# Layer 0's LayerNorm statistics: from 32-column fp32 sums that are spread afterwards to full fp32r products of split sums

## The chip, the core and the metric

The kernel runs on one core of a Trainium2 chip. The metric is device time in microseconds (us) of one launch, as the median of several runs. The core has five engines that work at the same time, each through its own instruction queue in order: TensorE (PE, matmuls, with weight loads beside them), VectorE (DVE), ScalarE (ACT), GpSimd (POOL) and SyncE (SP, which issues the transfers).

## The reference

The program is one inference step of a decoder with two layers, over 256 prompt tokens and 8 sample tokens, 264 in all, with 1024 features. Layer 0 is a gated short convolution, layer 1 block-sparse attention. Each layer has a wide input projection, a mixer, an output projection, and then a LayerNorm over the features of `alpha * x + mixer(x)`:

```python
def _layernorm(x, g, b):
    xf = x.astype(jnp.float32)
    mu = xf.mean(-1, keepdims=True)
    var = jnp.square(xf - mu).mean(-1, keepdims=True)
    return ((xf - mu) * lax.rsqrt(var + LN_EPS) * g + b).astype(x.dtype)

for i in range(DEPTH):            # DEPTH = 2
    ...                           # yp, ys: the mixer's output, after the output projection
    xp = _layernorm(DN_ALPHA * xp + yp, ln_g[i], ln_b[i])
    xs = _layernorm(DN_ALPHA * xs + ys, ln_g[i], ln_b[i])
```

The change is in the LayerNorm between layer 0 and layer 1.

## The kernel before

**Layout.** Activations lie with features on the 128 partitions and tokens along the row: `xf[:, m]` holds features 128m to 128m+127 of all 264 tokens, for m = 0 to 7. So a mean over features is a sum over 8 blocks and then over partitions, and the second part needs a matmul with a constant matrix.

**Slabs.** The weights come as slabs numbered 4 to 79, each 128 output columns by 1024 inputs. A slab is loaded (`load`, line 112, on SP), and split into a high part in the fp32r format (`hi`, line 124, on ACT) and the remainder (`lo`, line 129, on DVE). Activations are split in the same way into a pair of tiles, `pair[0]` or `pair[1]` (m0h, m0l, m1h, m1l in the profile). The product of a slab is 8 blocks of three matmuls (lines 136 to 138: high x high, high x low, low x high), accumulated in one of three PSUM tiles `acc`. Slabs 32 to 39 are layer 0's output projection; slabs 40 to 71 are layer 1's input projection, 40 to 47 of it q.

**Order.** PE's order is the program's order. The work of the other engines is hung into slots by hand: `at(n, phase, f)` adds `f` to slot n, and `begin(n)`, called ahead of slab n's matmuls, issues the slot's work in the order "dma", "pe", "s0", "hi", "lo", "s1a", "s1b", "s1", "s1c"; `split_late(n)` then issues the phases "hi3" and "lo3". Two tables, `hi_slot` and `lo_slot`, say in which slot a slab is split. Slabs 45 to 49 are split in the late phases. With each `lo` goes the `load` of the slab four places later in the list of slabs, since it takes the raw tile that `lo` frees. So for slab 45 `lo` carries `load(49)`, for slab 46 `load(50)`, for slab 47 `load(51)`.

**The norm of layer 0** (class `Norm`, object `ln`). As the output slabs come in, DVE adds them to `xf` (`evac`, line 280; a shift by block 0's mean is added too), ACT squares each block (`square`, line 301), ACT and DVE form the split pair of `gamma * x` (`cg_h`, line 501; `cg_l`, line 504), and POOL adds blocks 0 to 6 and their squares up in `sr` and `q` (`sums`, lines 308 and 309). `stats_mm` (line 317) then multiplies `sr`, `q`, block 7 and its square by an fp32 constant of 32 columns, in four quarters of 66 tokens, so that each quarter of the tokens has its mean and mean square on 32 partitions. `stats` makes `var`, the square root (line 330, ACT) and the reciprocal (line 331, DVE), all on 66 columns. `bcast_mm` (line 340) spreads them over all partitions by matmuls with a selection matrix, and `bcast` (lines 346 and 349) copies them out as two tiles of 264 columns: `ln.nd` (minus the mean) and `ln.rs` (one over the deviation).

**What uses the norm.** Layer 1 does not wait for it: for slabs 40 to 46 the matmuls run on the pair of `gamma * x`, with two extra columns for gamma and beta, and the norm is put on the result (`u_evac`, lines 574 to 577, on DVE; `u_fin` on ACT), which also frees the PSUM tile `acc`. From slab 47 on the matmuls take the normalised `x1`, in `pair[1]`, which DVE and ACT form block by block in slots 40 to 46 (`x1_norm`, lines 810 and 811; `x1_affine`; `x1_low`, line 819). Slots 40 and 41 are written out by hand. In slot 46 DVE rotates the sample tokens' q and copies it into `zq` (line 707); in slot 47, after half of its matmuls, PE multiplies the first cached keys by `zq` (`qk`, line 716: scores into `sd`).

Of the kernel before, what the change touches and what calls it, by code (L numbers as in the profile page):

```python
# [10 lines left out]
F32 = mybir.dt.float32  # L11
# [10 lines left out]
N = T + B  # L22
# [27 lines left out]
def build(tc, a):  # L50
# [3 lines left out]
    with ExitStack() as top:  # L54
# [91 lines left out]
        def run(n, phase):  # L146
            for f in hooks.pop((n, phase), []):
# [3 lines left out]
                   43: 36, 44: 37, 45: 40, 46: 40, 47: 43, 48: 45, 49: 46, 50: 47, 51: 48, 52: 48, 53: 49,  # L151
                   54: 49, 78: 74}
        lo_slot = {4: 3, 5: 3, 6: 3, 7: 4, 8: 5, 9: 5, 45: 40, 46: 41, 47: 44, 51: 49, 52: 49,
# [82 lines left out]
        onem = cp.tile([128, 2, 32], F32, name="onem")  # L236
        pool.memset(onem[:, 0], -1.0 / 1024)
        pool.memset(onem[:, 1], 1.0 / 1024)
        sel = cp.tile([128, 4, 128], F32, name="sel")[:, 0]
        pool.memset(sel, 0.0)  # L240
        for j in range(4):
            pool.memset(sel[32 * j:32 * j + 1], 1.0)
# [25 lines left out]

        G = N // 4

        class Norm:
# [38 lines left out]

            def stats_mm(self):
                self.mean = att_tile("ln0")
                self.e2 = att_tile("ln1")

                def acc(p, w, src, first, last):
                    for j in range(4):
                        pe.matmul(p[32 * j:32 * j + 32, 0:G], w, src[:, G * j:G * j + G],
                                  start=first, stop=last)
                acc(self.mean, onem[:, 0], self.sr, True, False)
                acc(self.e2, onem[:, 1], self.q, True, False)  # L320
                acc(self.mean, onem[:, 0], xf[:, 7], False, True)
                acc(self.e2, onem[:, 1], self.last_sq, False, True)

            def stats(self):
                self.st = self.t("st", 2 * G)
                var = self.t("var", G)
                act.copy(self.st[:, 0:G], self.mean[:, 0:G])
                act.activation(var, self.mean[:, 0:G], AF.Square)
                dve.tensor_sub(var, self.e2[:, 0:G], var)
                act.activation(var, var, AF.Sqrt, bias=epst)  # L330
                dve.reciprocal(self.st[:, G:2 * G], var)

            def bcast_mm(self):

                two = big_tile("lnb")
                ps = [two[:, 0:2 * G], two[:, 512:512 + 2 * G]] + \
                     [att_tile(f"lnb{i}")[:, 0:2 * G] for i in range(2)]
                for j in range(4):
                    q = np.s_[32 * j:32 * j + 32]
                    pe.matmul(ps[j], sel[q], self.st[q], start=True, stop=True)  # L340
                return two, ps

            def bcast(self, nm, src, c):
                two, ps = src
                t = self.t(nm)
                act.copy(t[:, 0:2 * G].rearrange("p (j r) -> p j r", j=2),
                         two.rearrange("p (j r) -> p j r", j=2)[:, :, G * c:G * c + G])
                for j in (2, 3):
                    act.copy(t[:, G * j:G * j + G], ps[j][:, G * c:G * c + G])
                return t  # L350
# [171 lines left out]
        for m in (6, 7):  # L522
            cg_l(m)
# [4 lines left out]
        with tc.tile_pool(name="l1", bufs=1) as p1, ExitStack() as late_pool:  # L528
# [448 lines left out]
            mm(ac2[0], 40, pair[0], range(0, 4), last=False)  # L977
            ln.stats_mm()
            ln.stats()
            split_late(40)  # L980
            mm(ac2[0], 40, pair[0], range(4, 7), first=False, last=False)
            begin(41, False)
            mm(ac2[1], 41, pair[0], range(0, 3), last=False)
            ps = ln.bcast_mm()
# [179 lines left out]
```

## Time and profile before

| | us |
|---|---|
| median of 3 runs (lowest to highest) | 280.36 (280.11 to 280.70) |
| the profiled execution | 280.45 |
| its span, first to last instruction | 278.7 |
| PE busy | 272.7 (98% of the span) |
| DVE busy | 195.6 (70%) |
| ACT busy | 155.3 (56%) |
| POOL busy | 59.8 (21%) |

The profile is of one execution. Lines of the trace in order of time give the start in us, the duration in us, the engine, the line of the kernel, the operation, output <- inputs, shapes and how often it came in a row; in brackets stands how long the engine had been idle before and what ended that. Lines of a group give the count, then the busy time in us, the mean of one in ns, and idle time before. Lines of a stretch give from:to, its length, and the busy time of the engine asked for. PEld is PE's weight load. Matmul durations overlap each other; the distance of two starts is what a matmul costs.

### The profile page before, as it was taken

How to read it: one execution, taken by the hardware profiler on the slowest of the kernel's cores; microseconds unless marked ns; L12 is line 12 of the kernel's file. 1: busy time of each engine (PE TensorE's matmuls, PEld its weight loads, DVE VectorE, ACT ScalarE, POOL GpSimd, SP SyncE). 2: the span in 40 equal slices, each digit the busy share in tenths (PEclk: the TensorE clock that was granted, in tenths of full speed). 3: DMA queues.
4: the chain of work that ended last, by engine and by line, in shares of the span. 5: the costliest groups of instructions: out<-in, count | busy, mean ns of one | idle time of the engine just before them, and what ended most of it. 6: DMA issues, size and time to landing. Idle time of an engine off the chain costs nothing.

```text
span 278.7 us, 6245 instructions
## 1 busy us (share of the span) xinstructions
PE 272.7 (98%) x2330; PEld 255.6 (92%) x2330; DVE 195.6 (70%) x377; ACT 155.3 (56%) x294; POOL 59.8 (21%) x130
## 2 busy tenths in 40 slices
PE   8999999999999999999999999999999999999992
PEld 5999999999999999999998997999959987988891
DVE  3868976655766768969999498498626384993745
ACT  4876564444655538557776495567746752571101
POOL 2110532020101102850311158411100030000212
PEclk9999999999999999999999999999999999999998
DMA  7985989999666876134025999999864995781012
GB/s 230 410 266 189 310 274 331 385 373 356 230 211 224 295 238 221 43 119 152 2 75 194 387 399 348 359 335 304 277 223 149 311 379 173 236 290 61 0 78 85
DMA packets 24495, 66.34 MB, mean 238 GB/s; under 512 B 3090, under 2 KB 6930, under 8 KB 24466
## 3 DMA queue, kind: packets, MB, share of 16 engines
q1 hardware_dynamic: 24178, 65.63, 67.4%
q8 instruction: 18, 0.29, 0.4%
q10 hardware_dynamic: 288, 0.33, 0.4%
q14 instruction: 11, 0.09, 0.1%
HBM read 61.55 MB, written 3.35 MB: 233 GB/s over the span
## 4 chain that ended last, share of the span: by engine, by line
PE 98%; DVE 1%; issue 0%
PE acc L136 24%; PE acc L138 24%; PE acc L137 24%; PE c L961 4%; PE sd L716 3%; PE dps L768 3%; PE acc L961 2%; PE acc L465 2%; PE acc L466 2%; PE acc L469 1%; PE so L1062 1%; PE warmp L80 1%; PE s L649 1%; PE o L688 1%; PE c1b L961 1%; PE c1c L961 1%
## 5 line engine op out<-in xcount | busy, mean ns | idle before, releaser
L124 ACT CAST hi<-raw 128x1024 fp32r<-128x1024 f32 x76 | 79.2, 1049 | 35.2 <-DMA raw<-w 22.1
L129 DVE TENSOR_TENSOR lo<-raw,hi 128x1024 fp32r<-128x1024 f32 x76 | 92.7, 1230 | 7.6 <-ACT hi L124 7.4
L138 PE MATMUL acc<-m0h,lo 128*128 128x264 f32 (+1 forms) x280 | 79.4, 284 | 0.0
L137 PE MATMUL acc<-m0l,hi 128*128 128x264 f32 (+1 forms) x280 | 79.3, 283 | 0.0
L136 PE MATMUL acc<-m0h,hi 128*128 128x264 f32 (+1 forms) x280 | 79.3, 283 | 0.0
L136 PE MATMUL acc<-m1h,hi 128*128 128x264 f32 x264 | 76.6, 290 | 0.0
L138 PE MATMUL acc<-m1h,lo 128*128 128x264 f32 x264 | 74.8, 283 | 0.0
L137 PE MATMUL acc<-m1l,hi 128*128 128x264 f32 x264 | 74.7, 283 | 0.0
L136 PEld LDWEIGHTS acc<-m0h,hi 128*128 128x128 f32 x280 | 52.7, 188 | 0.2
L138 PEld LDWEIGHTS acc<-m0h,lo 128*128 128x128 f32 x280 | 52.8, 189 | 0.0
L137 PEld LDWEIGHTS acc<-m0l,hi 128*128 128x128 f32 x280 | 52.7, 188 | 0.0
L136 PEld LDWEIGHTS acc<-m1h,hi 128*128 128x128 f32 x264 | 49.7, 188 | 1.7 <-issue 1.7
L137 PEld LDWEIGHTS acc<-m1l,hi 128*128 128x128 f32 x264 | 49.7, 188 | 0.1
L138 PEld LDWEIGHTS acc<-m1h,lo 128*128 128x128 f32 x264 | 49.7, 188 | 0.0
L421 POOL COPY uo<-up 128x10 f32<-128x10 f32 x8 | 8.0, 1002 | 66.8 <-DVE up L420 58.9
L657 DVE TENSOR_TENSOR s<-s,cst 128x256 f32<-128x256 f32 x8 | 3.4, 430 | 14.7 <-PE s L649 14.7
L799 DVE TENSOR_TENSOR gt<-z,q 128x256 f32<-128x256 f32 x8 | 3.4, 423 | 9.4 <-ACT z L796 9.4
L932 ACT ACTIVATE row<-row,epst 128x1 f32<-128x1 f32 x2 | 0.6, 295 | 16.6 <-DVE row L931 16.6
L666 ACT ACTIVATE P<-s,mx 128x128 f32<-128x128 f32 (+1 forms) x16 | 6.6, 416 | 5.6 <-DVE mx L660 5.6
L796 ACT ACTIVATE z<-acc 128x264 f32<-128x264 f32 x8 | 3.1, 391 | 11.4 <-PE acc L138 11.4
L628 POOL COPY vs<-vh 128x8 f32<-128x8 f32 x8 | 1.6, 204 | 34.9 <-ACT vh L627 34.9
L466 PE MATMUL acc<-m0l,hi 128*128 128x264 f32 x32 | 8.9, 306 | 0.0
(215 smaller groups left out, 415.4 us busy)
## 6 DMA issues: line engine op xcount, KB each, us to landing
raw<-w SPq DMA_DIRECT2D x76, 512.0 KB, 4.7
kv<-kc SPq DMA_DIRECT2D x32, 256.0 KB, 5.7
kv<-vc SPq DMA_DIRECT2D x16, 512.0 KB, 6.6
first<-first SPq DMA_DIRECT2D x6, 388.0 KB, 6.9
k_o<-kall SPq DMA_DIRECT2D x8, 132.0 KB, 5.1
v_o<-vh SPq DMA_DIRECT2D x8, 132.0 KB, 5.2
xf<-kall SPq DMA_DIRECT2D x16, 64.0 KB, 3.1
kall<-gb SPq DMA_DIRECT2D x2, 512.0 KB, 5.0
```

The source lines that it names most:

```text
L124: act.copy(his[n][sl], raws[n][sl])
L129: dve.tensor_sub(los[n][sl], raws[n][sl], his[n].bitcast(F32)[sl])
L136: pe.matmul(acc, wh, mh[:, k, 0:w], start=first and k == ks[0], stop=False)
L137: pe.matmul(acc, wh, ml[:, k, 0:w], start=False, stop=False)
L138: pe.matmul(acc, wl, mh[:, k, 0:w], start=False, stop=last and k == ks[-1])
L421: pool.tensor_copy(uo[:, f], up[:, T:N + 2])
L465: pe.matmul(accs[s], wh, mh, start=k == 0, stop=False)
L466: pe.matmul(accs[s], wh, ml, start=False, stop=False)
L666: act.activation(P[sl], s_ps[h][sl], AF.Exp, bias=mx[:, 2 + i:3 + i], scale=SCALE, accum_out=mx[:, 4 + i:5 + i])
L716: pe.matmul(s[32 * j:32 * j + 16, 0:256], zq[:, o:o + 16], kt, start=step == 0 and i == 0, stop=step == 3 and i == 3)
L768: pe.matmul(dps[0][32 * j:32 * j + 32, 512 * c:512 * c + 512], pm[b2][pg][:, j, :], kv_tiles[step, j][:, 512 * c:512 * c + 512], start=ste ...
L961: pe.matmul(acc, g[m][:, k, t], wide(d, k)[:, c0:c1], start=k == 0 and i == 0, stop=k == 7 and i == 2)
```

## The change

The statistics are formed on all 128 partitions at once, for all 264 tokens.

- POOL also adds block 7 and its square (`sums(7)`), and the two sums are split into fp32r high and low parts (`parts`: two copies on ACT, two subtractions on DVE), ahead of `cg_l(7)`.
- `stats_mm` is four matmuls of 264 columns with the constant `ones2` (-1/128 everywhere, there already): high and low part of the sum, then of the squares. They stand on PE after 7 blocks of slab 40 and 2 of slab 41 (27 matmuls); before, the sums stood after 4 blocks of slab 40 (12 matmuls), and the spreading matmuls 18 matmuls after them.
- `stats` works on 264 columns: a square, a fused multiply and subtract, the square root, a copy and the reciprocal. `bcast_mm`, `bcast` and the constants `onem` and `sel` go.
- `hi(45)` moves from slot 40 to 38 and `lo(45)` from 40 to 39; `hi(46)` moves from slot 40 to 41 and `lo(46)` from 41 to 43.

```diff
@@ -148,9 +148,9 @@
                 f()
 
         hi_slot = {4: 3, 5: 3, 6: 3, 7: 4, 8: 4, 9: 5, 10: 5, 11: 6, 38: 33, 39: 34, 40: 22, 41: 24, 42: 26,
-                   43: 36, 44: 37, 45: 40, 46: 40, 47: 43, 48: 45, 49: 46, 50: 47, 51: 48, 52: 48, 53: 49,
+                   43: 36, 44: 37, 45: 38, 46: 41, 47: 43, 48: 45, 49: 46, 50: 47, 51: 48, 52: 48, 53: 49,
                    54: 49, 78: 74}
-        lo_slot = {4: 3, 5: 3, 6: 3, 7: 4, 8: 5, 9: 5, 45: 40, 46: 41, 47: 44, 51: 49, 52: 49,
+        lo_slot = {4: 3, 5: 3, 6: 3, 7: 4, 8: 5, 9: 5, 45: 39, 46: 43, 47: 44, 51: 49, 52: 49,
                    53: 50, 54: 50, 39: 34}
 
         order = []
@@ -233,13 +233,6 @@
         pool.memset(onesf, 1.0)
         ones2 = cp.tile([128, 128], F32R, name="ones2")
         pool.tensor_scalar(ones2, onesf, -1.0 / 128, None, ALU.mult)
-        onem = cp.tile([128, 2, 32], F32, name="onem")
-        pool.memset(onem[:, 0], -1.0 / 1024)
-        pool.memset(onem[:, 1], 1.0 / 1024)
-        sel = cp.tile([128, 4, 128], F32, name="sel")[:, 0]
-        pool.memset(sel, 0.0)
-        for j in range(4):
-            pool.memset(sel[32 * j:32 * j + 1], 1.0)
 
         kv_tiles = {}
         KV = [("k", hh, b2) for hh in range(2) for b2 in range(2)] + \
@@ -266,8 +259,6 @@
                 sp.dma_start(t, a["vc"][page(2 * j + b2, c)].rearrange("o p e -> (o p) e"))
 
 
-        G = N // 4
-
         class Norm:
             def __init__(self, gi):
                 self.gi = gi
@@ -308,46 +299,35 @@
                     pool.tensor_tensor(self.sr, self.sr, xf[:, m], ALU.add)
                 pool.tensor_tensor(self.q, self.q, self.last_sq, ALU.add)
 
+            def parts(self):
+                self.part = [[lnp.tile([128, N], F32R, name=f"{c}{d}") for d in "hl"] for c in "sq"]
+
+                def high(i):
+                    act.copy(self.part[i][0], (self.sr, self.q)[i])
+
+                def low(i):
+                    dve.tensor_sub(self.part[i][1], (self.sr, self.q)[i], self.part[i][0].bitcast(F32))
+                self.sums(7)
+                high(0)
+                high(1)
+                low(0)
+                low(1)
+
             def stats_mm(self):
-                self.mean = att_tile("ln0")
-                self.e2 = att_tile("ln1")
-
-                def acc(p, w, src, first, last):
-                    for j in range(4):
-                        pe.matmul(p[32 * j:32 * j + 32, 0:G], w, src[:, G * j:G * j + G],
-                                  start=first, stop=last)
-                acc(self.mean, onem[:, 0], self.sr, True, False)
-                acc(self.e2, onem[:, 1], self.q, True, False)
-                acc(self.mean, onem[:, 0], xf[:, 7], False, True)
-                acc(self.e2, onem[:, 1], self.last_sq, False, True)
+                self.mean = att_tile("ln0")[:, 0:N]
+                self.e2 = att_tile("ln1")[:, 0:N]
+                for p, part in zip((self.mean, self.e2), self.part):
+                    for i, c in enumerate(part):
+                        pe.matmul(p, ones2, c, start=i == 0, stop=i == 1)
 
             def stats(self):
-                self.st = self.t("st", 2 * G)
-                var = self.t("var", G)
-                act.copy(self.st[:, 0:G], self.mean[:, 0:G])
-                act.activation(var, self.mean[:, 0:G], AF.Square)
-                dve.tensor_sub(var, self.e2[:, 0:G], var)
-                act.activation(var, var, AF.Sqrt, bias=epst)
-                dve.reciprocal(self.st[:, G:2 * G], var)
-
-            def bcast_mm(self):
-
-                two = big_tile("lnb")
-                ps = [two[:, 0:2 * G], two[:, 512:512 + 2 * G]] + \
-                     [att_tile(f"lnb{i}")[:, 0:2 * G] for i in range(2)]
-                for j in range(4):
-                    q = np.s_[32 * j:32 * j + 32]
-                    pe.matmul(ps[j], sel[q], self.st[q], start=True, stop=True)
-                return two, ps
-
-            def bcast(self, nm, src, c):
-                two, ps = src
-                t = self.t(nm)
-                act.copy(t[:, 0:2 * G].rearrange("p (j r) -> p j r", j=2),
-                         two.rearrange("p (j r) -> p j r", j=2)[:, :, G * c:G * c + G])
-                for j in (2, 3):
-                    act.copy(t[:, G * j:G * j + G], ps[j][:, G * c:G * c + G])
-                return t
+
+                self.nd, self.rs = self.t("n"), self.t("r")
+                act.activation(self.rs, self.mean, AF.Square, scale=0.125)
+                dve.scalar_tensor_tensor(self.rs, self.e2, -0.125, self.rs, ALU.mult, ALU.subtract)
+                act.activation(self.rs, self.rs, AF.Sqrt, bias=epst)
+                act.activation(self.nd, self.mean, AF.Copy, scale=0.125)
+                dve.reciprocal(self.rs, self.rs)
 
             def gcol(self, m):
                 return col(3 + 2 * self.gi, m)
@@ -519,8 +499,9 @@
 
         out_slabs(ln, 32, g, cg)
         cg_h(7)
-        for m in (6, 7):
-            cg_l(m)
+        cg_l(6)
+        ln.parts()
+        cg_l(7)
 
         l0.close()
 
@@ -974,21 +955,17 @@
 
             ac2 = [acc_tile() for _ in range(2)]
             begin(40, False)
-            mm(ac2[0], 40, pair[0], range(0, 4), last=False)
+            mm(ac2[0], 40, pair[0], range(0, 7), last=False)
+            begin(41, False)
+            mm(ac2[1], 41, pair[0], range(0, 2), last=False)
             ln.stats_mm()
             ln.stats()
             split_late(40)
-            mm(ac2[0], 40, pair[0], range(4, 7), first=False, last=False)
-            begin(41, False)
-            mm(ac2[1], 41, pair[0], range(0, 3), last=False)
-            ps = ln.bcast_mm()
-            ln.nd = ln.bcast("n", ps, 0)
-            ln.rs = ln.bcast("r", ps, 1)
             split_late(41)
             for m in (0, 1):
                 x1_norm(m)
                 x1_affine(m)
-            mm(ac2[1], 41, pair[0], range(3, 7), first=False, last=False)
+            mm(ac2[1], 41, pair[0], range(2, 7), first=False, last=False)
             for i in range(2):
                 mm(ac2[i], 40 + i, pair[0], range(7, 8), first=False)
                 at(42, "s0", u_evac, i, ac2[i])
```

## The prediction

> **What bounds the kernel now.** I read the chain of work that ended last first, then the rows of TensorE (PE), VectorE (DVE), ScalarE (ACT) and GpSimd (POOL) in order of time around layer 0's norm (118 to 146 us).
>
> ```profile
> PE 98%; DVE 1%; issue 0%
> 122.94 0.28 PE L138 MATMUL acc<-m0h,lo 128*128 128x266 f32 x1
> 123.15 0.32 PE L317 MATMUL ln<-sr,onem 128*32 128x66 f32 x8
> 123.75 0.39 PE L136 MATMUL acc<-m0h,hi 128*128 128x266 f32 x1
> 123.98 0.29 PE L137 MATMUL acc<-m0l,hi 128*128 128x266 f32 x1
> ...
> 125.97 0.28 PE L138 MATMUL acc<-m0h,lo 128*128 128x266 f32 x1
> 126.18 0.51 PE L340 MATMUL lnb<-st,sel 32*128 32x132 f32 x8
> 126.62 0.39 PE L136 MATMUL acc<-m0h,hi 128*128 128x266 f32 x1
> 126.85 0.28 PE L137 MATMUL acc<-m0l,hi 128*128 128x266 f32 x1
> ...
> 128.94 0.28 PE L136 MATMUL acc<-m0h,hi 128*128 128x266 f32 x1
> ...
> 143.68 0.28 PE L136 MATMUL acc<-m1h,hi 128*128 128x264 f32 x1
> 145.22 3.65 PE L716 MATMUL sd<-kv,zq 128*16 128x256 f32 x64
> ```
>
> PE is the chain, with hardly a gap, so whatever leaves PE in this stretch shortens the kernel unless another engine then makes PE wait. The row at 128.94 opens slab 42 and that at 143.68 slab 47: 120 matmuls in 14.74 us, 0.123 us each. The engine that could make PE wait is DVE:
>
> ```profile
> 124.79 0.57 DVE L331 RECIPROCAL st<-var 128x66 f32<-128x66 f32 x1 [0.42 <-ACT var L330]
> 125.73 2.36 DVE L129 TENSOR_TENSOR lo<-raw,hi 128x1024 fp32r<-128x1024 f32 x2 [0.37 <-ACT hi L124]
> 128.01 0.42 DVE L810 TENSOR_TENSOR xf<-xf,n 128x264 f32<-128x264 f32 x1
> 128.53 0.43 DVE L811 TENSOR_TENSOR xf<-xf,r 128x264 f32<-128x264 f32 x1
> 139.94 1.22 DVE L129 TENSOR_TENSOR lo<-raw,hi 128x1024 fp32r<-128x1024 f32 x1
> 141.07 0.15 DVE L574 COPY uv<-acc 128x2 f32<-128x2 f32 x1
> 141.26 0.49 DVE L576 SCALAR_TENSOR_TENSOR t<-n,uv,acc 128x264 f32<-128x264 f32 x1
> 143.59 0.27 DVE L707 COPY zq<-qs 128x16 f32<-128x16 f32 x2
> 128.01:143.86 15.85, 14.87 (x45) 1.00 0.31 100
> ```
>
> The last line is DVE's busy time from the first row that needs the norm's result (128.01) to the end of the copies into `zq` (143.59 + 0.27 = 143.86): 14.87 of 15.85 us. No row in it names a releaser; what is missing are steps between dependent instructions. So from 128.01 on DVE works down a queue without waiting for anybody, and PE's scores at 145.22 read `zq`, which was ready only 1.36 us earlier. That is the slack to watch.
>
> **The change, part by part.**
>
> PE, removed. The 32-column sums: 122.94 to 123.75 is 0.81 instead of 0.12, and the next step 0.23 instead of 0.12: 0.80 us. The spreading matmuls: 125.97 to 126.62 is 0.65, again followed by 0.23: 0.64 us. Together 1.44 us.
>
> PE, added. Four matmuls of 264 columns with `ones2`, of the kind that runs at 0.123 a step: 0.49 us. If nothing waits, PE gains 0.95 us. They come after 27 slab matmuls instead of 12: 121.59 (where slab 40 starts in the row below) + 27 x 0.123 = 124.91.
>
> ```profile
> 121.59 0.28 PE L136 MATMUL acc<-m0h,hi 128*128 128x266 f32 x1
> 115.09 1.49 DVE L129 TENSOR_TENSOR lo<-raw,hi 128x1024 fp32r<-128x1024 f32 x1
> 118.09 1.22 DVE L129 TENSOR_TENSOR lo<-raw,hi 128x1024 fp32r<-128x1024 f32 x1
> 119.22 0.98 DVE L504 SCALAR_TENSOR_TENSOR m0l<-xf,cst,m0h 128x264 fp32r<-128x264 f32 x1
> 120.13 0.42 DVE L280 SCALAR_TENSOR_TENSOR xf<-xf,acc 128x264 f32<-128x264 f32 x1
> 122.14 0.49 DVE L504 SCALAR_TENSOR_TENSOR m0l<-xf,cst,m0h 128x264 fp32r<-128x264 f32 x1
> 118.31 1.60 POOL L308 TENSOR_TENSOR sr<-sr,xf 128x264 f32<-128x264 f32 x1 [0.20 <-DVE xf L280]
> 119.87 0.95 POOL L309 TENSOR_TENSOR q<-q,sqm 128x264 f32<-128x264 f32 x1
> 120.78 0.75 POOL L308 TENSOR_TENSOR sr<-sr,xf 128x264 f32<-128x264 f32 x1
> 121.50 0.75 POOL L309 TENSOR_TENSOR q<-q,sqm 128x264 f32<-128x264 f32 x1
> 120.64 0.42 ACT L301 ACTIVATE sqm<-xf 128x264 f32<-128x264 f32 x1 [1.52 <-DVE xf L280]
> 124.41 0.35 ACT L330 ACTIVATE var<-var,epst 128x66 f32<-128x66 f32 x1 [0.29 <-DVE var L329]
> L124 ACT CAST hi<-raw 128x1024 fp32r<-128x1024 f32 x76 | 79.2, 1049 | 35.2 <-DMA raw<-w 22.1
> L816 ACT CAST m1h<-xf 128x264 fp32r<-128x264 f32 x8 | 3.3, 413 | 0.3
> L819 DVE TENSOR_TENSOR m1l<-xf,m1h 128x264 fp32r<-128x264 f32 x8 | 3.0, 424 | 0.0
> ```
>
> POOL and the moved `lo(45)`. A POOL sum takes 0.75 us alone (120.78), 1.60 beside a DVE `lo` (118.31); it ended 0.60 after that `lo` (118.09 + 1.22 = 119.31; 119.91). DVE's next two-input product took 0.98 instead of 0.49 and ended 0.29 after the sum (120.20), and the next sum 0.63 after that (120.83). They take turns. The Trainium skill ("SBUF — State Buffer", "SBUF: two separate sides") says that GpSimd and a VectorE instruction with two SBUF inputs hold a shared port pair in turn, for a whole instruction each; the trace agrees (1.60 against 0.75), and without turns the sum below would be that of the first rival. Before, the `sums(6)` pair at 120.78 ran at 0.75 each. Now `lo(45)` stands there, behind the evacuation at 120.13: held by the sum at 119.87 as the `lo` at 115.09 (1.49) was, it ends at 121.9. Then by turns: sum `sr` 122.5, `cg_l(6)` 122.8, sum `q` 123.4. The new `sums(7)` follow with DVE idle: 124.15 and 124.87.
>
> The splits. `high` of q: one hand-over (0.1) and a 0.41 copy (the L816 row): 125.38. `low` 0.43 (the L819 row) and 0.03: 125.84. The last stats matmul starts at 125.89 instead of 124.91 + 3 x 0.123 = 125.28: PE waits 0.61, and slab 42 opens 0.34 ahead of before.
>
> The statistics. Matmul end 126.17; DVE's fused subtract 0.42 (as L280): 126.62; the square root, 0.35 on 66 columns, about 0.54 on 264: 127.19. Then the reciprocal, 264 columns instead of 66 and still on DVE ahead of the norm:
>
> ```profile
> L671 DVE RECIPROCAL mx<-mx 128x2 f32<-128x2 f32 x8 | 1.3, 161 | 0.0
> L935 DVE RECIPROCAL row<-row 128x1 f32<-128x1 f32 x2 | 0.3, 156 | 0.0
> L329 DVE TENSOR_TENSOR var<-ln,var 128x66 f32<-128x66 f32 x1 | 0.2, 226 | 0.5 <-ACT var L328 0.5
> ```
>
> (566 - 156) / 65 = 6.3 ns a column, so 0.156 + 263 x 0.0063 = 1.81 us. Low end: 0.57 plus 198 columns at what an ordinary instruction adds, (0.424 - 0.226) / 198 = 1 ns: 0.77. High end: four times 0.566 = 2.26. I take 1.81, since the three reciprocals lie on one line. The Trainium skill ("VectorE: DVE Perf Modes", "First, the fixed hardware budget") gives the divide a repeat count of 8; at its 0.96 GHz that is an estimate of 8.3 ns a column, 2.2 us, which the slope of 6.3 ns does not bear out. So the reciprocal ends at 129.03; `x1_norm(0)` starts at 128.96 and its second product at 129.41 instead of 128.53: DVE's queue is 0.88 late.
>
> `lo(46)`. Before, both moved `lo` ran in 125.73 to 128.09, ahead of the norm. Now `lo(46)` stands in slot 43, inside the full stretch: 139.94 to 141.07, 1.13 us. At `zq` DVE is 0.88 + 1.13 = 2.01 late.
>
> The sum. `zq` is ready at 145.87, and PE's scores start at about 145.92 instead of 145.22. PE alone would be there at 144.88, so it waits 1.04, of which some 0.5 already at slab 47's start: its accumulator is the one that the L576 at 141.26 frees, now at 143.76, and PE is there at 143.34. Sum: -0.95 + 0.61 + 1.04 = **+0.70 us**. The scores themselves are 3.65 us of PE work that needs nothing more of DVE's queue, and in them the rest of its lateness is taken up.
>
> ```profile
> 126.98 1.46 SPq L112 DMA_DIRECT2D raw<-w  x2
> ```
>
> At no cost: `hi(45)` (1.05 on ACT) goes into the idle 1.52 that ACT has before 120.64; without that gap it would hold up the squares, and POOL's sums behind them, by up to 1.05. The evacuations of `n` and `r` that go, and POOL's memsets at the start, end no wait of PE. The two loads of this last row are issued by the moved `lo`: `load(49)` moves from 127 to 122, `load(50)` from 128 to 139. SP works in order, but the next in its queue, `load(51)`, waits for `lo(47)` in slot 44 anyway. Slab 50's raw tile is first read in slot 47, four microseconds later; if it landed after that, `hi(50)` would wait on ACT, and PE needs it three slabs further on.
>
> **The rivals.**
>
> 1. POOL's sums are not held up (not slower). If the `sums(6)` pair ends at 122.25 as now, `sums(7)` end at 123.85, everything up to `zq` comes 1.02 earlier, and the sum is -0.32: 280.0 us as a median. For it: the pair ran at 0.75 each. Against: `lo(45)` is queued right behind the evacuation whose result POOL waits for. It decides once q's last sum ends before 124.2 (0.70 earlier).
> 2. The reciprocal streams (0.77): `zq` late by 0.97, and PE's own 0.34 is all that is left: 280.0 us. Against: a column costs 6 ns already between 1, 2 and 66.
> 3. The reciprocal costs four times 0.566: +0.45, so +1.15: 281.5 us. For it: 8.6 ns a column at 66 columns, start-up counted in. Against: the line through 1, 2 and 66.
> 4. The whole PE gain arrives, -0.95: 279.4 us. It needs r by about 127.4, 1.6 us earlier than I have it: POOL free and a cheaper reciprocal, or room in DVE's queue that its rows do not show (its 0.98 of gaps would hold most of `lo(46)`).
>
> **How the numbers follow.** The profiled execution took 280.45 us (span 278.7 and 1.75 around it), 0.09 above the median 280.36. 280.45 + 0.70 is 281.15, as a median 281.06; I say 281.1. Under 0.2% (0.56 us) a measurement of this kernel can't tell from no change. Chances: forecast 0.45, rival 1 0.18, rival 2 0.10, rival 3 0.12, rival 4 0.15. The forecast lies just above 280.92, the bound of "slower"; I put a quarter of its chance under it. So slower is 0.34 + 0.12 = 0.46, same 0.11 + 0.28 = 0.39, faster 0.15. The range goes from rivals 1 and 2 to rival 3, 279.9 to 281.6, and leaves rival 4 out.
>
> **What would show it.** Right: POOL's `sums(6)` sum over 1.4 us beside the `lo` near 120.5; the last stats matmul half a microsecond or more behind its place; a RECIPROCAL of 128x264 at about 1.8; `x1_norm(0)` near 129; the `zq` copies ending near 145.9, the scores starting on them, and PE idle before slab 47 or the scores. Wrong: PE without a gap from slab 42 to the scores, and these ahead of 145.2. What would upset it most is an earlier r, or a DVE queue that runs faster than its rows before.

## The result, and the profile after

The changed kernel takes 281.97 us (median of 6 runs, 281.62 to 282.84); the kernel before, beside it, 280.24 (279.91 to 280.77, 6 runs). The ratio is 1.0066, interval 1.0046 to 1.0085: 1.73 us slower, where +0.70 was forecast. The profiled execution of the changed kernel is the slowest of its six (282.84, span 281.1), so the trace shows somewhat more loss than the median: 2.4 us of span.

The first view is the timeline of the changed kernel around the norm, all engines.

```profile
120.61 1.44 DVE L129 TENSOR_TENSOR lo<-raw,hi 128x1024 fp32r<-128x1024 f32 x1
120.92 1.74 POOL L299 TENSOR_TENSOR sr<-sr,xf 128x264 f32<-128x264 f32 x1
122.63 0.96 POOL L300 TENSOR_TENSOR q<-q,sqm 128x264 f32<-128x264 f32 x1
123.53 0.76 POOL L299 TENSOR_TENSOR sr<-sr,xf 128x264 f32<-128x264 f32 x1
124.24 0.76 POOL L300 TENSOR_TENSOR q<-q,sqm 128x264 f32<-128x264 f32 x1
125.05 0.29 PE L321 MATMUL ln<-sh,ones 128*128 128x264 f32 x1
...
125.48 0.43 DVE L309 TENSOR_TENSOR ql<-q,qh 128x264 fp32r<-128x264 f32 x1 [0.19 <-ACT qh L306]
...
125.97 0.39 PE L321 MATMUL ln<-ql,ones 128*128 128x264 f32 x1
126.19 0.29 PE L136 MATMUL acc<-m0h,hi 128*128 128x266 f32 x1
127.49 1.80 DVE L330 RECIPROCAL r<-r 128x264 f32<-128x264 f32 x1 [0.58 <-ACT r L328]
129.21 0.37 DVE L791 TENSOR_TENSOR xf<-xf,n 128x264 f32<-128x264 f32 x1
129.61 0.43 DVE L792 TENSOR_TENSOR xf<-xf,r 128x264 f32<-128x264 f32 x1
```

`lo(45)` now stands where the `sums(6)` pair is, and the first sum takes 1.74 us. The four statistics matmuls reach from 125.05 to the next slab matmul at 126.19, 1.14 us for 0.49 of work: PE waits 0.65. The reciprocal of 264 columns takes 1.80, and the norm's first block starts at 129.21. Slab 40 itself opens 0.13 later than before (121.72), so 0.13 of every later time is none of this.

The same timeline from slab 46's end to the second scores, PE and DVE:

```profile
137.97 1.22 DVE L129 TENSOR_TENSOR lo<-raw,hi 128x1024 fp32r<-128x1024 f32 x1
...
143.38 0.28 PE L138 MATMUL acc<-m0h,lo 128*128 128x266 f32 x1
143.49 0.49 DVE L557 SCALAR_TENSOR_TENSOR t<-n,uv,acc 128x264 f32<-128x264 f32 x1
144.13 0.36 PE L136 MATMUL acc<-m1h,hi 128*128 128x264 f32 x1 [0.47 <-DVE t L557]
...
145.82 0.26 DVE L688 COPY zq<-qs 128x16 f32<-128x16 f32 x2
146.11 4.08 PE L697 MATMUL sd<-kv,zq 128*16 128x256 f32 x64 [0.29 <-issue]
150.12 0.39 PE L136 MATMUL acc<-m1h,hi 128*128 128x264 f32 x1
...
170.58 2.35 PE L697 MATMUL sd<-kv,zq 128*16 128x256 f32 x38
173.39 1.89 PE L697 MATMUL sd<-kv,zq 128*16 128x256 f32 x26 [0.47 <-DMA kv<-kc]
175.20 0.39 PE L136 MATMUL acc<-m1h,hi 128*128 128x264 f32 x1
```

and the kernel before, the end of its first scores and its second ones:

```profile
148.80 0.39 PE L136 MATMUL acc<-m1h,hi 128*128 128x264 f32 x1
...
169.26 3.65 PE L716 MATMUL sd<-kv,zq 128*16 128x256 f32 x64
172.84 0.39 PE L136 MATMUL acc<-m1h,hi 128*128 128x264 f32 x1
```

Three losses can be read off, each as a distance of two starts. The first scores start 0.76 later (146.11 against 145.22, less the 0.13). They take 4.01 us instead of 3.58 (146.11 to 150.12; 145.22 to 148.80): 0.43. The second scores take 4.62 instead of 3.58 (170.58 to 175.20; 169.26 to 172.84): 1.04, and there PE waits for a tile of cached keys. 0.76 + 0.43 + 1.04 = 2.23; with the 0.13 at the start and 0.03 after 175, the span's 2.39. Of the 1.04, 0.47 is named as idle; the 26 matmuls behind that wait also take 1.81 us (173.39 to 175.20), where 26 of the 64 before take 1.45 (3.58 x 26 / 64).

### The profile page after: what moved, and what is told of

Read it like the earlier page. It is cut to its first block, busy times and chain, and to the rows that moved or that the text cites. A ratio compares the mean times of both kernels' runs of the same rounds, so it can differ in the third digit from the quotient of the medians.

```text
span 281.1 us, 6163 instructions
## 1 busy us (share of the span) xinstructions
PE 272.9 (97%) x2294; PEld 256.3 (91%) x2294; DVE 198.2 (71%) x379; ACT 155.6 (55%) x290; POOL 63.0 (22%) x125
## 4 chain that ended last, share of the span: by engine, by line
PE 78%; DVE 10%; DMA 4%; issue 3%; ACT 2%; POOL 0%; SPq 0%; DVEq 0%; ACTq 0%; POOLq 0%
PE acc L136 19%; PE acc L138 18%; PE acc L137 18%; PE c L942 4%; PE dps L749 3%; DMA kv<-kc 2%; PE sd L697 2%; DMA first<-first 2%; PE acc L942 2%; DVE lo L129 1%; PE so L1039 1%; PE s L630 1%; PE o L669 1%; DVE m0l L484 1%; PE acc L445 1%
## 5 line engine op out<-in xcount | busy, mean ns | idle before, releaser
L401 POOL COPY uo<-up 128x10 f32<-128x10 f32 x8 | 9.0, 1124 | 66.1 <-DVE up L400 60.1
L409 DVE SCALAR_TENSOR_TENSOR t<-up,cst,t 128x256 f32<-128x256 f32 x8 | 3.9, 483 | 7.4 <-ACT t L408 7.4
```

The costliest lines, as they stand in the source:

```text
L401: pool.tensor_copy(uo[:, f], up[:, T:N + 2])
L409: dve.scalar_tensor_tensor(t1[:, 0:T], up[:, 1:T + 1], col(1, f), t0, ALU.mult, ALU.add)
```

## The experiments

All runs are read by the same distances of PE starts. The columns: how much later the `zq` copies start, measured from slab 40's start; how much later the first scores start; how long the first and the second scores take (3.58 each before); how much later the second scores end, all from slab 40's start in the profiled execution, in us; then the median, and its ratio to the kernel before on the same chip, with the interval.

| kernel | zq | scores start | first | second | end | median | ratio |
|---|---|---|---|---|---|---|---|
| the change | +2.10 | +0.76 | 4.01 | 4.62 | +2.23 | 281.97 | 1.0066 [1.0046, 1.0085] |
| 1 slots only | +0.66 | +0.18 | 3.58 | 3.73 | +0.33 | 280.61 | 1.0023 [1.0004, 1.0043] |
| 2 short reciprocal | +0.85 | -0.28 | 3.80 | 4.50 | +0.85 | 280.73 | 1.0024 [1.0015, 1.0033] |
| 3 keys first | +2.10 | +0.75 | 3.99 | 4.94 | +2.53 | 282.60 | 1.0090 [1.0073, 1.0107] |
| 4 no reciprocal | -0.03 | -0.28 | 3.58 | 3.57 | -0.29 | 279.77 | 0.9992 [0.9981, 1.0003] |
| 5 before, keys first | +0.02 | +0.01 | 3.57 | 3.58 | 0.00 | 280.09 | 0.9994 [0.9985, 1.0004] |
| 6 lo(49) earlier | +2.09 | +0.74 | 3.92 | 4.35 | +1.85 | 281.66 | 1.0053 [1.0039, 1.0067] |
| 7 no reciprocal, lo(45) back | +0.41 | -0.93 | 3.92 | 4.32 | +0.14 | 280.41 | 1.0001 [0.9988, 1.0014] |
| 8 lo(45) back | +2.68 | +1.33 | 3.93 | 3.79 | +2.70 | 282.46 | 1.0081 [1.0068, 1.0094] |
| 9 keys a slot earlier | +2.06 | +0.72 | 3.92 | 3.58 | +2.61 | 282.64 | 1.0069 [1.0045, 1.0092] |
| 10 before, the same | +0.02 | 0.00 | 3.58 | 3.58 | +0.62 | 280.39 | 1.0005 [0.9988, 1.0021] |
| 11 combination | -0.28 | -0.45 | 3.58 | 3.58 | -0.23 | 280.62 | 1.0006 [0.9987, 1.0025] |
| 12 before, DVE held up | +2.07 | +0.72 | 3.92 | 4.66 | +2.40 | 283.78 | 1.0112 [1.0089, 1.0134] |
| 13 one load less | +2.06 | +0.72 | 3.92 | 3.57 | +1.04 | 281.17 | 1.0042 [1.0029, 1.0054] |
| 14 before, one load less | 0.00 | 0.00 | 3.58 | 3.58 | -0.01 | 279.94 | 0.9992 [0.9981, 1.0004] |
| 15 statistics later | +0.15 | -0.94 | 3.67 | 3.84 | -0.62 | 279.79 | 0.9994 [0.9979, 1.0008] |
| 16 = 15, one load less | +0.16 | -0.95 | 3.71 | 3.58 | -0.83 | 279.28 | 0.9970 [0.9959, 0.9980] |
| 17 = 15, five raw tiles | +0.14 | -0.95 | 3.67 | 4.23 | -0.22 | 280.26 | 1.0008 [0.9994, 1.0022] |
| 18 change, five raw tiles | +2.09 | +0.75 | 3.92 | 4.96 | +2.45 | 282.30 | 1.0069 [1.0051, 1.0087] |

Slab 40 starts at different times in the profiled executions, from 0.26 earlier to 0.11 later even in 5, 10 and 14, which are the kernel before up to there, and up to 0.75 earlier and 1.14 later (12) in the others. So a median need not follow the column before it to a few tenths; what the prediction is about is read from the columns, what a kernel is worth from the median.

### Which part of DVE's lateness counts

**1, slots only.** The kernel before, with the changed `hi_slot` and `lo_slot` (45: 38, 46: 41 and 45: 39, 46: 43).

> The kernel before with only the four slots of the change (hi and lo of slabs 45 and 46 moved), statistics as before. Theory A (DVE's queue from the norm to slab 47 is full, and late work in it delays first the key scores of slab 47, then the loads behind it on SP): the norm starts some 0.35 us earlier, lo(46) adds 1.13 in slot 43, so the zq copies come about 0.8 late, inside their 1.36 of slack; the key loads after slab 47 come up to 0.8 late, just their margin of about 0.8 at slab 54. So 280.2 to 280.6 us against about 280.3 before. Theory B (the move of lo(46) alone costs most of the loss): 281.3 or more.

Measured 280.61, ratio 1.0023. The moved `lo` alone make `zq` 0.66 late and cost 0.33 at the second scores' end.

**2, short reciprocal.** The change, with the reciprocal on a quarter of the columns; the others keep the square root.

```diff
-                dve.reciprocal(self.rs, self.rs)
+                dve.reciprocal(self.rs[:, 0:66], self.rs[:, 0:66])
```

> The changed kernel with the reciprocal on the first 66 columns only (the other columns keep the square root). Theory A: DVE's queue is 1.24 us earlier from the norm on, the zq copies are at about 144.6, so the first key scores wait for nothing or 0.1, and the key loads behind lo(49) come about 1.0 late instead of 2.2, so the second scores wait 0.2 to 0.6: 280.0 to 280.7 us. Theory B (the loss is PE's own wait in front of the statistics matmuls and the transfers, whatever DVE does): within 0.2 of the changed kernel, 281.8.

Measured 280.73. `zq` comes 1.25 earlier than in the change (0.85 late), which is 1.80 - 0.57, the two reciprocals' rows: DVE's queue hands a duration on in full. But though PE now arrives at the scores 0.28 early and `zq` is there, the first scores take 3.80 and the second 4.50; the keys are waited for:

```profile
168.59 2.35 PE L697 MATMUL sd<-kv,zq 128*16 128x256 f32 x38
171.27 1.89 PE L697 MATMUL sd<-kv,zq 128*16 128x256 f32 x26 [0.34 <-DMA kv<-kc]
```

So the wait for keys does not come by way of `zq`, which is there in time; it comes already when DVE's queue is 0.85 late.

**3, keys first.** The change, with `load(53)`, which goes with `lo(49)`, issued two slots later, behind the keys of slot 48.

```diff
-                at(ls, "lo" + late, load, order[i + 4])
+                at(*((48, "s0") if n == 49 else (ls, "lo" + late)), load, order[i + 4])
```

> The changed kernel with one load moved on SP: load(53) behind the four transfers of the first key tiles of slot 48 instead of ahead of them, so that these do not wait for lo(49). Theory A: nothing changes up to the first key scores (0.76 and the 0.43 in them stay), the key transfers start at about 150.3 instead of 152.5, the second key scores run without a wait and give back their 1.0 us: about 281.0 us. Theory B (the second scores are late for another reason, such as the transfers' bandwidth): 281.8 to 282.0.

Measured 282.60, ratio 1.0090. The first keys now go out at 150.19, as early as in the kernel before (150.24; 152.47 in the change), and yet the second scores take 4.94. The order of these issues is not what delays the keys.

**4, no reciprocal.** The change, with number 3's edit and the square root and reciprocal as one ACT operation.

```diff
-                act.activation(self.rs, self.rs, AF.Sqrt, bias=epst)
                 act.activation(self.nd, self.mean, AF.Copy, scale=0.125)
-                dve.reciprocal(self.rs, self.rs)
+                act.activation(self.rs, self.rs, AF.Abs_reciprocal_sqrt, bias=epst)
...
-        at(34, "s1", table, AF.Sqrt)
+        at(34, "s1", table, AF.Abs_reciprocal_sqrt)
```

> The changed kernel with one over the root in one ScalarE operation (its table is loaded in slot 34, where that of the square root was), the copy of the mean ahead of it, no reciprocal on DVE, and the load order of the experiment with the keys first. Theory A: r is there at about 127.5, DVE's queue starts about 0.6 earlier than in the kernel before and with lo(46) is 0.5 late at zq, inside the slack; PE keeps its 0.35 to 0.4 ahead, and the second scores wait for nothing: 279.8 to 280.1 us, 0.3 below before. Theory B (PE's own wait and the transfers): 281 or more.

Measured 279.77. ACT and DVE in its timeline:

```profile
126.45 0.52 ACT L329 ACTIVATE r<-r,epst 128x264 f32<-128x264 f32 x1 [0.49 <-DVE r L327]
127.00 0.44 DVE L791 TENSOR_TENSOR xf<-xf,r 128x264 f32<-128x264 f32 x1 [0.25 <-ACT r L329]
```

The operation takes 0.52, as the square root did in the change (row at 126.94), `zq` is not late, and both scores have their 3.58: what the change lost beyond the PE sum goes with DVE's lateness. (Two things differ here, but number 3's edit alone gained nothing in the change, nor in the kernel before, number 5.) What arrives is 0.29, PE's gain less its wait at the statistics (0.34 in the prediction).

### Is one late load the link

**5, before, keys first**: number 3's edit in the kernel before.

> The kernel before with only load(53) put behind the four transfers of the first key tiles on SP. Theory A2 (the key scores of slab 54 are late because the ring of raw slab tiles is: a late load(53) makes hi(53) and lo(53) late, these make load(57) late, and the last key transfers stand behind that load on SP; the transfers have no spare time from 150 to 172 us to catch up): load(53) goes out about 1.3 us later, the first scores are as before, the second ones wait: 0.4 to 1.0 us slower than before, with PE waiting in them. Theory B2 (the second scores are late only because the first key transfers start late): no slower than before, since these start earlier here.

Measured 280.09: no change.

**6, lo(49) earlier.** The change, with `49: 46` in `lo_slot` instead of 47, so that its load goes out a slot earlier.

> The changed kernel with lo(49) one slot earlier (46 instead of 47, so ahead of the evacuation of slab 46), which sends load(53) about 1 us earlier. Theory A2: the first scores stay late as in the changed kernel, the second ones wait less: 0.4 to 1.0 us faster than the changed kernel, 280.8 to 281.5 us. Theory B2 or a late start that nothing makes up: 281.7 to 282.0.

Measured 281.66. The second scores take 4.35 instead of 4.62 in the trace: a part of the wait, not the wait. By the medians it can't be told from the change (the intervals overlap).

**7, no reciprocal and lo(45) back.** Number 4's operation, `45: 40` in `lo_slot`, loads in their order.

> The changed kernel with one over the root in one ScalarE operation, no reciprocal on DVE, loads in the order of the changed kernel, and lo(45) in slot 40, behind the statistics, out of the way of POOL's sums. Theory A: POOL's sums of block 6 run at 0.75 each, PE waits 0.1 or less at the statistics matmuls, DVE's queue starts about 0.8 ahead of the kernel before and is 0.3 late at zq, inside the slack: PE keeps 0.8 to 0.95, 279.1 to 279.4 us against 280.1 before. Rival: PE's wait only moves to the accumulators or the scores, 279.8 or more.

**8, lo(45) back.** The change, with `45: 40` in `lo_slot`.

> The changed kernel with lo(45) in slot 40, behind the reciprocal, instead of slot 39. Theory A: POOL's sums of block 6 take 0.75 each instead of 1.74 and 0.96, the last sum ends 1.0 earlier, PE's wait of 0.6 at the statistics matmuls goes, but lo(45) now stands between the reciprocal and the norm, so DVE's queue starts where it did and the first scores are as late: the time of the changed kernel, 281.6 to 282.0. Rival (PE's wait at the statistics is a loss of its own): 281.2 to 281.3.

7 measured 280.41, 8 measured 282.46. With `lo(45)` away from the sums these run at 0.75, and the statistics matmuls at their pace (number 8, timeline):

```profile
120.68 0.75 POOL L299 TENSOR_TENSOR sr<-sr,xf 128x264 f32<-128x264 f32 x1
...
124.82 0.29 PE L321 MATMUL ln<-sh,ones 128*128 128x264 f32 x1
...
125.19 0.28 PE L321 MATMUL ln<-ql,ones 128*128 128x264 f32 x1
```

PE's wait at the statistics is gone, and yet 8 is no faster than the change (282.46, the intervals overlap; the second scores end 2.70 late instead of 2.23): its `lo(45)` now lies in DVE's full stretch and `zq` is 2.68 late. In 7 PE reaches the scores 0.93 early and gives it back in both scores (3.92, 4.32).

### Do earlier keys cure it, and does lateness suffice

**9, keys a slot earlier.** The change, with the fourth, fifth and sixth of the six later key tiles (two transfers each) a slot ahead.

```diff
-KV_AT = (8, 8, 9, 10, 11, 12, 13, 14, ...
+KV_AT = (8, 8, 9, 9, 10, 11, 13, 14, ...
```

> The changed kernel with the last three of the six key tiles of the second scores sent one slot earlier on SP (slots 49, 50, 51 instead of 50, 51, 52), so ahead of a slab load each. Theory A3 (the second scores wait because DVE's late queue makes the lo of slabs 49 to 52 and so the slab loads 53 to 56 late, and the last keys stand behind later loads of that ring, in transfers that are busy all the time): the first scores stay late, the second ones run in 3.58 without a wait: 1.0 us faster than the changed kernel, 280.8 to 281.0 us. Theory B3 (the wait has another cause): 281.7 to 282.

**10, before, the same**: that edit in the kernel before.

> The kernel before with the same three key tiles one slot earlier. All theories: its second scores wait for nothing already, so no change, 280.0 to 280.3 us; slower only if the slab loads behind them come too late for PE.

9 measured 282.64, 10 measured 280.39. The second scores of 9 are whole, but two slabs ahead of them now wait:

```profile
163.44 0.39 PE L136 MATMUL acc<-m1h,hi 128*128 128x264 f32 x1 [0.36 <-ACT kall L573]
...
167.27 0.39 PE L136 MATMUL acc<-m1h,hi 128*128 128x264 f32 x1 [0.67 <-ACT kall L573]
```

These slabs' accumulator is freed by ACT, and ACT stands behind `hi`, which waits for a slab's transfer (ACT idle for 3.01 and 1.64 us). Keys that go first make the slabs late; the end is 2.61 late instead of 2.23. In the trace of 10 one slab waits in the same way (0.36 at 165.10) and the end is 0.62 late, but its median does not show it.

**11, combination.** Number 7 with number 9's order of keys, and heads 0 to 3 rotated and copied to `zq` a slot earlier.

> A candidate for a faster kernel: the changed kernel with one over the root in one ScalarE operation, lo(45) in slot 40, the keys one slot earlier as in the two experiments above, and the rotation and copy of the first four heads' q into zq in slot 45 instead of 46. Theory A3: PE keeps its 0.95 up to the first scores, zq is there 0.9 us or more ahead of them, so they take 3.58, and so do the second: 279.2 us against 280.1 before. Rival: the first or second scores still take 3.8 to 4.3: 279.6 to 280.3.

Measured 280.62, ratio 1.0006: no gain, though its profiled execution has both scores at 3.58.

**12, before, DVE held up.** The kernel before, its statistics untouched, with two reciprocals on a constant that nobody reads, in slot 43 of DVE's queue.

```diff
+        late = cp.tile([128, N], F32, name="late")
+        pool.memset(late, 1.0)
...
+            at(S + 3, "lo3", dve.reciprocal, late, late)
+            at(S + 3, "lo3", dve.reciprocal, late[:, 0:32], late[:, 0:32])
```

> The kernel before, statistics, slots and loads as they were, with two more operations on DVE at the end of slot 43, reciprocals of a constant tile of 264 and of 32 columns, 2.1 us that nobody reads. Theory A3 (the loss of the change is nothing but DVE's lateness there): the zq copies come 2.1 late, the first scores start 0.75 late and take 0.4 longer, the second take 0.9 to 1.0 longer: 2.1 us slower, 282.1 to 282.3 us. Rival (a part of the loss lies in the new statistics themselves): 281.5 or less.

Measured 283.78. PE and DVE in its timeline:

```profile
138.03 2.18 DVE L144 RECIPROCAL late<-late 128x264 f32<-128x264 f32 x2
...
147.08 3.99 PE L718 MATMUL sd<-kv,zq 128*16 128x256 f32 x64 [0.28 <-issue]
...
171.72 2.35 PE L718 MATMUL sd<-kv,zq 128*16 128x256 f32 x38
174.56 1.89 PE L718 MATMUL sd<-kv,zq 128*16 128x256 f32 x26 [0.49 <-DMA kv<-kc]
```

`zq` 2.07 late gives the pattern of the change in all three places, with nothing else of it there. (Of the 3.94 us by which its profiled span is longer than before's, 1.54 lie outside the stretch: 1.14 ahead of slab 40, where no row names a new wait of PE, and 0.40 behind the second scores. Their cause is open, so the median of 12 is no price of the lateness; the columns are.)

### What hands the lateness on to the keys

The rows of stretches, 122 to 170 us, first before, then after. Behind the length stand the busy times of PE, PEld, DVE, ACT and POOL with their counts and the granted clock; the last two columns are the mean busy share of the transfer engines and the GB/s.

```profile
122.00:128.00 6.00, 6.00 (x80) 5.50 (x79) 4.18 (x7) 4.32 (x13) 0.24 (x1) 1.00 0.03 5
128.00:150.00 22.00, 22.00 (x214) 20.05 (x214) 20.81 (x57) 14.89 (x27) 4.05 (x13) 1.00 0.30 94
150.00:160.00 10.00, 10.00 (x85) 10.00 (x84) 5.71 (x11) 5.85 (x10) 1.06 (x3) 1.00 0.93 347
160.00:170.00 10.00, 10.00 (x94) 9.56 (x96) 9.13 (x19) 8.36 (x15) 6.40 (x13) 1.00 1.04 400
```

```profile
122.00:128.00 6.00, 5.91 (x46) 5.49 (x45) 3.26 (x8) 3.12 (x8) 3.00 (x4) 1.00 0.28 96
128.00:150.00 22.00, 21.24 (x204) 20.45 (x202) 20.91 (x55) 15.07 (x27) 3.48 (x12) 1.00 0.14 49
150.00:160.00 10.00, 10.00 (x84) 9.88 (x82) 7.41 (x13) 4.96 (x8) 2.39 (x4) 1.00 0.81 291
160.00:170.00 10.00, 10.00 (x85) 10.00 (x84) 7.91 (x16) 9.04 (x16) 4.99 (x11) 1.00 1.04 405
```

GB/s times us, added up: by 160 the kernel before has moved 0.03 + 2.07 + 3.47 = 5.57 MB since 122, the changed one 0.58 + 1.08 + 2.91 = 4.56. That is 1.0 MB less, and from 160 on both move 400 GB/s with no room: 2.5 us. (PE itself comes to the second scores 1.19 late, so only the rest can show there as a wait.) A load is issued when DVE's `lo` frees a raw tile, so a late DVE starts the transfers late, and where they run full nothing makes it up. The first four key transfers for the second scores, issued behind such a load, go out 2.23 later (first before, then after):

```profile
150.24 1.93 SPq L263 DMA_DIRECT2D kv<-kc  x4
152.47 1.93 SPq L256 DMA_DIRECT2D kv<-kc  x4
```

**13, one load less.** The change, without slab 53's transfer (its split reads slab 52's raw tile).

```diff
         def load(n):
+            if n == 53:
+                raws[53] = raws[52]
+                return
```

> The changed kernel, with slab 53 not loaded: its split reads slab 52's raw tile (so slab 53's products are those of 52). From there on there are 0.5 MB less to transfer, and each later load finds its raw tile free one slab sooner. If the wait of 1.04 us in the second scores is the transfers' (they run full from 150 to 172 us and start 2.2 us late): the first scores stay late (0.76 at their start, 0.4 in them), the second ones shrink from 4.6 to 3.6 us, the end of the second scores is 1.2 late instead of 2.2, and the time is about 281.0. If DVE's lateness reaches the second scores by another way (the keys' issue behind DVE's splits, the evacuations): no change, 281.9.

**14, before, one load less.**

> The kernel before with the same transfer left out. Both theories: nothing in the kernel before waits for keys or for a raw tile long enough to show, so 280.2 within 0.3; a gain of over 0.5 would say that the transfers bound the kernel before as well, and that the reading of the run beside it is worth nothing.

13 measured 281.17, 14 measured 279.94. The wait for keys is gone from 13 (second scores, 169.69 on), and the first scores are as late as in the change:

```profile
145.32 3.99 PE L700 MATMUL sd<-kv,zq 128*16 128x256 f32 x64 [0.29 <-issue]
...
169.69 3.65 PE L700 MATMUL sd<-kv,zq 128*16 128x256 f32 x64
```

In the kernel before the same omission moves nothing in the stretch. The omission also lets the first keys go out earlier (149.49), but that alone did not help in number 3; the bytes are what is new. In the traces the end of the second scores is 1.19 less late (2.23 and 1.04), and what remains is the first scores' loss. By the medians it is 0.80 of the 1.73 us (281.97 - 281.17), with 0.92 left (0.81 to 1.5 by the interval); this split is rough, since the two were measured on different chips and the intervals of the ratios overlap.

**15, statistics later.** Number 4, with the statistics matmuls after 4 blocks of slab 41 (33 slab matmuls, not 27).

> The changed kernel with the square root and reciprocal made in one ScalarE operation (the run with 279.77), and the four statistics matmuls after 4 blocks of slab 41 instead of 2 (33 slab matmuls instead of 27). Their operands come at 3.3 to 4.25 us after slab 40's start; at 4.07 PE hardly waits for them, which frees the 0.56 it waits there. r is no later, so zq stays where it is, and scores that start 0.56 earlier still find it 0.8 ahead. If PE bounds the rest: 0.3 + 0.55 early at the end of the second scores, 279.3. If the keys' transfers bound the second scores (they do not move): the second scores take 0.3 to 0.5 longer, 279.6 to 279.8, no better than without the move.

**16: number 15 with number 13's edit.**

> The kernel beside it without slab 53's transfer. If the transfers are what holds the second scores there: 0.85 early at the end of the second scores and 279.3 even where the kernel beside it is at 279.7. If that one already has 279.3: the same.

15 measured 279.79, 16 measured 279.28. PE no longer waits at the statistics and is 0.94 early at the first scores. 15 gives some back in both scores, 3.67 and 3.84 instead of 3.58; 16 keeps it and is the only one faster for certain, 0.9970 [0.9959, 0.9980], with a transfer left out. PE's gain is thus real, and the transfers stand in its way.

**17 and 18, five raw tiles.** Number 15 (without number 3's edit) and the change, with `bufs=5` for the raw tiles, and `load(order[i + 5])` with each `lo` (the sums' parts in tiles `sqm`, `n` and `r`, free at that time, make the room).

> The norm without the reciprocal and with the statistics after 33 slab matmuls (the run with 279.79), with a fifth raw tile, so that each load is issued one split earlier; the sums' parts lie in tiles of the norm that are free then, which makes the room. If the late issue of the loads is what delays the keys: the transfer share between 128 and 150 us rises, the second scores take 3.6 us, 0.8 early at their end, about 279.3, as with the transfer left out. If it is the number of bytes between 150 and 172 us in itself, or if the loads now stand ahead of the keys in the queue: the second scores stay at 3.8 or more, 279.8 or above.

> The changed kernel with a fifth raw tile in the same way; nothing is left out. If the late issue of the loads makes the wait in the second scores: these go from 4.6 to 3.6 us and the rest stays (first scores 0.76 late and 0.4 longer): about 1.1 late, 281.2 as with slab 53's transfer left out. If not: 281.9.

17 measured 280.26, 18 measured 282.30: no help, so the expectation of a cure by earlier issue fell. (17 differs from 15 in the order of loads too; 18 differs from the change by the buffer alone.) In the stretches of 18:

```profile
128.00:150.00 22.00, 21.25 (x204) 20.44 (x203) 20.88 (x56) 14.63 (x27) 3.48 (x12) 1.00 0.15 50
150.00:160.00 10.00, 10.00 (x86) 10.00 (x85) 9.74 (x18) 7.22 (x13) 4.96 (x6) 1.00 0.90 311
160.00:170.00 10.00, 10.00 (x85) 9.94 (x83) 7.62 (x15) 7.82 (x13) 4.74 (x11) 1.00 1.03 401
170.00:173.00 3.00, 2.42 (x40) 1.06 (x38) 2.60 (x2) 1.55 (x3) 2.82 (x4) 1.00 1.07 416
```

The idle time before 150 is not filled: each `lo` still issues one load, only of a later slab. The last keys are issued no later than before, and land later (transfer issues between 163.5 and 166 us, first the kernel before, then 18; the last column is us to landing):

```profile
kv<-kc SPq DMA_DIRECT2D x2, 256.0 KB, 5.7
```

```profile
kv<-kc SPq DMA_DIRECT2D x2, 256.0 KB, 8.7
```

In number 13, with one transfer less ahead of them, the last keys are issued at 164.28 and land after 5.8. It is the bytes ahead of the keys between 150 and 173 us that count, not the issue.

## Why the prediction was wrong in size

**Right, step by step.** POOL's sum was held to 1.74 (forecast: over 1.4), q's last sum ended at 125.00 (124.87), PE waited 0.65 (0.61), the reciprocal took 1.80 (1.81), the norm's first block came at 129.21 (128.96), the `zq` copies ended at 146.08, 145.95 without the start's 0.13 (145.87), and the first scores started 0.76 late (+0.70 was the sum). Rivals 1 to 4 all fell by their own conditions: the last sum did not end before 124.2, the reciprocal took neither 0.77 nor 2.26, and it ended at 129.29, not by 127.4. The Trainium skill ("SBUF — State Buffer", "SBUF: two separate sides") has the turns of GpSimd and VectorE for the shared port pair; numbers 8 and the change bear it out as a pair, 0.75 without the `lo` beside the sum and 1.74 with it. The Trainium skill's repeat count of 8 for the divide ("VectorE: DVE Perf Modes", "First, the fixed hardware budget") would have given the estimate of 2.2 us; the 1.80 measured decides for the slope.

**Wrong: "in them the rest of its lateness is taken up".** The sum ended at the start of the first scores. Number 12 shows what a DVE queue late by 2.07 at `zq` costs by itself: 0.72 there, and 1.68 more by the end of the second scores. Two terms are missing.

The larger is in "At no cost: ... The two loads". I followed the two loads that change slots, and looked only at whether the slab's own raw tile comes in time. But all loads behind hang on DVE's `lo`, the transfers run full from 150 us on (0.93 and 1.04 of the engines in the kernel before already), and the second scores' keys are the last of that stretch. Their slack is a fraction of a microsecond: with `zq` 0.66 late the second scores take 3.73 (number 1), with 0.85 already 4.50 (number 2, where PE also comes 0.28 early). Price: 1.04 us of the profiled execution, about 0.80 of the median (13 against the change, roughly).

The smaller is in "The scores themselves are 3.65 us of PE work". Their length depends on how far `zq` is ahead of PE. Ends of the `zq` copies against the scores' start, in the profiled executions: 1.36, 0.88 and 1.1 us ahead (before, 1 and 4) give 3.58; 0.27 and 0.25 (15 and 16) 3.67 and 3.71; 0.23 (2) 3.80; 0.02 (7) and all where PE waits 3.92 to 4.01. So a wait in front of these 64 short matmuls costs 0.34 to 0.43 more than its own length. The trace puts the idle time down to issue. One thing differs in the rows, the scores' weight loads (first before, then after):

```profile
L716 PEld LDWEIGHTS sd<-kv,zq 128*16 128x16 f32 x64 | 1.8, 97 | 1.5
L697 PEld LDWEIGHTS sd<-kv,zq 128*16 128x16 f32 x64 | 3.5, 96 | 0.6 <-issue 0.5
```

64 loads of the same length overlap each other into 1.8 us of busy time when `zq` is early, and only into 3.5 when it is late (3.3 in number 2, 3.1 in 15). That goes with the longer scores; why they do not close up again is not shown.

The PE gain of 0.95 less 0.61 was right as well: it arrives where DVE is in time (number 4: 0.29 at the second scores' end; the ratio's interval does not exclude none). That 15, with PE's wait at the statistics gone too, is no faster than 4, while 16 is, is the same second bound: the transfers are close behind PE.

Open are the cause of the 0.34 to 0.43 in the first scores, the 1.54 us of number 12 outside the stretch, and why the median of 11 is no better than before's when its profiled execution, slab 40 0.75 earlier, has no loss left.

## What to carry to other kernels

An engine whose queue is full and that is late by d at one consumer is late by about d at everything that it releases behind it. Before a slack swallows it, follow the queue to the transfers that it lets go, and ask whether the transfer engines have room to catch up: in a stretch at 400 GB/s and a share of 1.0 they have none, and one more buffer moves no byte out of that stretch.

To test whether bytes or issue order bound such a place, leave one transfer out in both kernels: it took the wait away here, where changes of order (3, 6, 9) and of buffers (17, 18) had moved, trimmed or lengthened it.

A serial operation on a busy engine was better removed than hidden here: the reciprocal's 1.80 us went into a 0.52 us operation of ACT, which had a square root there anyway. That undid the loss; against the kernel before it is no sure gain (0.9992, interval up to 1.0003).

## What the runs showed of the hardware

- The reciprocal costs 1.80 us for 264 columns, 0.57 for 66 and 0.16 for 1 or 2: 6.3 ns a column, on one line.
- ACT's one-operation reciprocal square root takes 0.52 us for 264 columns, as its square root does (0.52).
- Transfers stay near 400 GB/s when pressed (400, 405, 401 and 416 in the stretches shown); the time from issue to landing of a 256 KB key transfer grows with what is queued, 3.6 us at 152.47 and 6.5 at 166 in the changed kernel, 8.7 in number 18.
- 64 matmuls of 16 columns take 3.58 us when their small operand lies ready 0.88 us or more ahead, 3.67 to 3.80 at 0.23 to 0.27, and 3.92 to 4.01 when it comes just in time.
